# A two-layer hybrid attention and FFN kernel: tile addresses set apart modulo 128 bytes, query-key products alternated between row halves, the first compression matrix used unsplit, and another opening order

## The chip, the cores and the metric

The kernel runs on one core of a Trainium2 chip. The metric is the device time of one execution in microseconds, taken as the median over several runs. The profile is of one execution on the chip; PE is TensorE's matmul row, PEld its weight loads, DVE VectorE, ACT ScalarE, POOL GpSimd and SP SyncE.

## The reference, cut to what matters

Two layers act on 256 tokens of width 1024, in float32:

```python
for l in range(DEPTH):
    h = rmsnorm(x, norm_mix_g[l]); proj = h @ w_in[l]
    # a: 24 heads of 64 in three dilation groups, banded causal attention, merged by log-sum-exp
    out_a = dilated_mixer(qa, ka, a_qkv[:, :, 2])
    # b: keys and values compressed over 32 tokens: gelu(flat @ cmp_w1) @ cmp_w2
    out_b = nsa_mixer(qb, k_cmp, v_cmp, k_sel, v_sel, k_win, v_win, b_gate)
    gate = sigmoid(merge)
    x = x + (gate0 * (out_a @ w_proj_a[l]) + gate1 * (out_b @ w_proj_b[l])) @ w_out[l]
    h = rmsnorm(x, norm_ffn_g[l]); g_in, u = split(h @ w_up[l])
    x = x + (silu(causal_dwconv(g_in, ...)) * u) @ w_down[l]
```

`cmp_w1[l, kv]` is a 2048 x 256 matrix for the keys (kv = 0) and one for the values (kv = 1). The output is the last x.

## The kernel before, in words

All weights lie in one stream of 512 KB halves; two halves are a unit (L42 lists the units in their order). SP loads each half into one of five `raw` tiles (L204, L206). For a unit, ACT casts the half to float32r as `hi` (L232) and DVE subtracts to get `lo` (L233). Activations are split in the same way, so that a product is three float32r matmuls: hi by hi, lo by hi, hi by lo (`mm3`, L283, and `feat_major`, L358). Each has its own weight load (PEld) of 128 columns. PE runs its program in the order in which the code emits it.

The input projections (`chunk_in`, L434) load tokens of `hT` as weights and stream 512 columns (280 in chunk c11) of the unit: 24 matmuls a unit, as L284, L285 and L286. The merge units (L927), both `proj` products (L972 to L974), `out_proj` (L985), `ffn_up` (L1001) and `ffn_down` (L1051) load the unit's columns as weights and stream 256 tokens: 48 matmuls a unit (L936 to L938, L972 to L974, L363, L1062 to L1064). A layer has 9 chunks c0 to c8 and c10, c11, bq of two units each, 8 merge, 4 proj, 4 out, 22 up, 11 down and 4 compression (w1) units.

Attention is written as generators (`job_a`, `job_b`, `job_cmp1`, `job_cmp2`, `rope_run`) that `tick` (L268) moves on by one step after each half of a projection unit, so that their instructions fall between the projections' matmuls. `chunk_in` calls `post_fn`, which starts `rope_run`, then `tick`. In `rope_run` (L411) the key path yields twice (L420) before the scaling by POOL's power (L368); its `fin` transposes the result on PE (`rope_b`, L474 after the copy L471).

`job_a` (L589) computes for head `lo` (partitions 0 to 63) all query-key products (`qk`, L606: L608, L609, L614), yields, takes the masked maxima on DVE (L603), and then does the same for head `up` (partitions 64 to 127). `col_pair` (L556) multiplies probabilities by values for two heads in turn, which write to PSUM partitions 0 to 63 and 64 to 127 (L560).

`job_cmp1` (L763) builds the compression input `Fv`, splits it into `F` (hi and lo side by side), and `w1_unit` (L793) multiplies F by hi and lo of each w1 unit: 16 matmuls of 256 columns a unit (L806, L807), four units a layer, placed after units 5, 6, 8 and 10 of the chunks.

The opening (L1072 on): SP issues gain, x in three parts and the halves of unit 0, then in `attention_layer` misc, ropec, cossin, gr, post, w2t; then the next halves. `feed` (L299) permutes each 128-token half of a feature block of x into token order, scales it into `hT` (two ACT instructions L310, two DVE L311), squares it (ACT L314, L317) and adds the square to a sum (POOL L319). Before the second unit of c10, `rstd_col` (L331) is emitted, whose matmul L334 needs the finished sum (`fin`, L327).

**Addresses.** The pools hand out SBUF in the order in which tiles are first asked for, each size rounded up to 32 bytes. Adding them up: `hT`, `raw`, and the `hi` and `lo` tiles of the shared pool `com` begin 96 bytes past a multiple of 128, `oTb` too; `oTa` at 0; the FFN's `u` and `act` at 32. In the FFN every third unit (`ffn_turn`, L209) takes `hi` and `lo` from the FFN's pool, at 32; the others take those of `com`, at 96. So the weight tile and the streamed tile of a matmul begin 64 bytes apart modulo 128 in two of three FFN units, 32 apart with `oTa`, and at the same place everywhere else.

The key line of each part:

```python
hi = pool.tile([P, UW], F32R, name="hi", bufs=nb)          # L222, com or the FFN's pool
T.matmul(s1[:, c0:c0 + P], qT[r, g, tok], kT[r, g, tok], start=True, stop=True)   # L614
T.matmul(o, F[:, c0:c0 + P], hi[:, j], start=jj == 0, stop=False)                # L806
```

## Time and profile before

| | us |
|---|---|
| median of 3 runs | 1004.22 (1000.14 to 1005.84) |
| the profiled execution's own time | 1000.91 |
| its span, first to last instruction | 999.2 |
| PE busy | 972.5 (97%) |
| DVE busy | 772.7 (77%) |
| ACT busy | 603.6 (60%) |
| POOL busy | 147.4 (15%) |

A row of a timeline has the start in us, the length in us of the merged run, engine, line, operation, `out<-in`, shapes and the count; in brackets the idle time of the engine before it and what ended it. The end of a matmul is modelled, so rows overlap: the time that a matmul takes from the engine is read from start to start. A window's row has each engine's busy time, the granted TensorE clock as a share of 2.4 GHz, the DMA share and GB/s.

### The profile page before, as it was taken

Reading aid. Unit: us, or ns where it says so; the run is one execution under the profiler, and the core shown is the slowest. Engines: PE = TensorE matmul, PEld = TensorE weight load, DVE = VectorE, ACT = ScalarE, POOL = GpSimd, SP = SyncE. Lnnn points to the kernel's source line nnn. Section 1 sums busy time; section 2 is a strip of 40 time slices with the busy share of each in tenths; the row PEclk is TensorE's granted clock in tenths of the full one; section 3 lists DMA queues with packets and bytes.
Section 4 is the critical chain, followed back from the end, with each engine's and each line's share of the span. In section 5 each row is a group of like instructions: output and inputs, shape, how many; then the busy total and the mean of one; then the engine's idle time right before and its main releaser. Section 6 shows DMA issues by size and latency. Waiting matters only on the chain.

```text
span 999.2 us, 18707 instructions
## 1 busy us (share of the span) xinstructions
PE 972.5 (97%) x7154; PEld 894.0 (89%) x7154; DVE 772.7 (77%) x1628; ACT 603.6 (60%) x1219; POOL 147.4 (15%) x164
## 2 busy tenths in 40 slices
PE   5899999999999999999998999999999999999998
PEld 3778888888999999999987788888899999999998
DVE  6799777887679898886478987787875898988742
ACT  6779666758456555555456886675665555555531
POOL 2241111203002111110112300121210021111100
PEclk9999999999999999999998999999999999999999
DMA  6644345534356566555454433563354465565660
GB/s 206 209 150 146 130 148 190 168 108 148 127 170 212 174 205 193 189 187 193 160 162 148 148 127 128 172 208 109 103 177 160 148 226 179 186 195 190 196 205 22
DMA packets 47897, 164.90 MB, mean 165 GB/s; under 512 B 6080, under 2 KB 7616, under 8 KB 47808
## 3 DMA queue, kind: packets, MB, share of 16 engines
q1 hardware_dynamic: 46656, 162.66, 50.1%
q8 instruction: 56, 0.92, 0.4%
q10 hardware_dynamic: 1152, 1.05, 0.3%
q14 instruction: 33, 0.27, 0.1%
HBM read 162.64 MB, written 1.05 MB: 164 GB/s over the span
## 4 chain that ended last, share of the span: by engine, by line
PE 81%; DVE 10%; ACT 6%; issue 2%; POOL 1%; DMA 1%; SPq 0%; DVEq 0%; ACTq 0%; POOLq 0%
PE acc L363 25%; PE acc L284 6%; PE acc L286 6%; PE acc L285 6%; PE acc L1062 4%; PE acc L1064 4%; PE acc L1063 4%; DVE lo L233 3%; PE acc L936 3%; PE acc L938 3%; PE att L560 3%; PE acc L937 3%; PE att L565 2%; PE acc L972 2%; PE acc L973 2%
## 5 line engine op out<-in xcount | busy, mean ns | idle before, releaser
L233 DVE TENSOR_TENSOR lo<-raw,hi 128x1024 fp32r<-128x1024 f32 (+1 forms) x308 | 386.3, 1274 | 62.6 <-ACT hi L232 60.7
L232 ACT CAST hi<-raw 128x1024 fp32r<-128x1024 f32 (+1 forms) x308 | 310.2, 1039 | 176.8 <-issue 49.2
L363 PE MATMUL acc<-u,hi 128*128 128x256 f32 x1376 | 240.9, 279 | 0.0
L363 PEld LDWEIGHTS acc<-u,hi 128*128 128x128 f32 x1376 | 210.0, 189 | 0.1
L363 PE MATMUL acc<-u,lo 128*128 128x256 f32 x688 | 191.8, 279 | 0.0
L284 PE MATMUL acc<-hi,hT 128*128 128x512 f32 (+1 forms) x384 | 154.7, 403 | 9.4 <-ACT hi L232 9.4
L286 PE MATMUL acc<-lo,hT 128*128 128x512 f32 (+1 forms) x384 | 151.2, 394 | 0.7 <-DVE lo L233 0.5
L285 PE MATMUL acc<-hi,hT 128*128 128x512 f32 (+1 forms) x384 | 150.2, 391 | 0.0
L363 PEld LDWEIGHTS acc<-u,lo 128*128 128x128 f32 x688 | 130.1, 189 | 0.0
L1064 PE MATMUL acc<-act,lo 128*128 128x256 f32 x352 | 97.8, 278 | 0.0
L1063 PE MATMUL acc<-act,hi 128*128 128x256 f32 x352 | 97.8, 278 | 0.0
L1062 PE MATMUL acc<-act,hi 128*128 128x256 f32 x352 | 97.8, 278 | 0.0
L284 PEld LDWEIGHTS acc<-hi,hT 128*128 128x128 f32 x384 | 73.8, 192 | 23.5 <-ACT hi L232 9.4
L286 PEld LDWEIGHTS acc<-lo,hT 128*128 128x128 f32 x384 | 73.8, 192 | 17.9 <-DVE lo L233 3.2
L285 PEld LDWEIGHTS acc<-hi,hT 128*128 128x128 f32 x384 | 73.9, 192 | 13.0 <-issue 0.3
L936 PE MATMUL acc<-hT,hi 128*128 128x256 f32 x256 | 74.3, 290 | 0.0
L938 PE MATMUL acc<-hT,lo 128*128 128x256 f32 x256 | 72.7, 284 | 0.0
L937 PE MATMUL acc<-hT,hi 128*128 128x256 f32 x256 | 72.3, 282 | 0.0
L1062 PEld LDWEIGHTS acc<-act,hi 128*128 128x128 f32 x352 | 66.5, 189 | 0.0
L1064 PEld LDWEIGHTS acc<-act,lo 128*128 128x128 f32 x352 | 66.5, 189 | 0.0
L1063 PEld LDWEIGHTS acc<-act,hi 128*128 128x128 f32 x352 | 66.5, 189 | 0.0
L1034 POOL TENSOR_TENSOR z<-z,rb 128x512 f32<-128x512 f32 x22 | 30.5, 1386 | 207.2 <-DVE z L1033 207.2
(212 smaller groups left out, 1783.9 us busy)
## 6 DMA issues: line engine op xcount, KB each, us to landing
raw<-in_ws_dram SPq DMA_DIRECT2D x300, 512.0 KB, 4.5
raw<-in_ws_dram SPq DMA_DIRECT2D x8, 280.0 KB, 4.3
out_dram<-x ACTq DMA_DIRECT2D x8, 128.0 KB, 2.2
gr<-in_g_rope_dram SPq DMA_DIRECT2D x2, 384.0 KB, 5.7
masks<-in_mask_dram SPq DMA_DIRECT2D x1, 576.0 KB, 4.9
x<-in_x_dram SPq DMA_DIRECT2D x2, 256.0 KB, 4.3
x<-in_x_dram SPq DMA_DIRECT2D x1, 512.0 KB, 7.5
w2t<-in_w_dram SPq DMA_DIRECT2D x2, 128.0 KB, 4.8
```

Source lines behind the costliest of these rows:

```text
L232: A.copy(h, r)
L233: V.tensor_sub(l, r, h.bitcast(F32))
L284: T.matmul(o, a_hi, b_hi, start=first, stop=False)
L285: T.matmul(o, a_lo, b_hi, start=False, stop=False)
L286: T.matmul(o, a_hi, b_lo, start=False, stop=last)
L363: return [lambda a=a: T.matmul(a[0], a[1], a[2], start=a[3], stop=a[4]) for a in todo]
L936: T.matmul(o, hi[:, k, ms], hT[:, 0, k], start=k == 0, stop=False)
L937: T.matmul(o, hi[:, k, ms], hT[:, 1, k], start=False, stop=False)
L938: T.matmul(o, lo[:, k, ms], hT[:, 0, k], start=False, stop=k == 7)
L1062: T.matmul(ps, hi[:, c], act[:, 0, k], start=k == 0, stop=False)
L1063: T.matmul(ps, hi[:, c], act[:, 1, k], start=False, stop=False)
L1064: T.matmul(ps, lo[:, c], act[:, 0, k], start=False, stop=k == NFT - 1)
```

## The change

1. **Addresses.** `warm` is added, misc is widened from 72 to 96 floats, mhalf is asked for after the `raw` tiles, `db` gets six buffers, `pad` tiles of 64 bytes are added, some tiles are asked for in another order, and the scratch at the foot of SBUF shrinks to 1024 bytes. Added up in the same way, all of these streams begin at multiples of 128: `hT`, `raw`, `u`, `act`, `oTa`, `oTb`, `qS`; `hi` and `lo` of both pools and `kS` begin at 64 past one.
2. **Query-key products.** They alternate between the two row halves, matmul by matmul; the own-group products come first, the dilated ones after a yield.
3. **First compression matrix.** A w1 unit now holds four row blocks of both matrices. It is not split: its float32 `raw` halves are streamed (256 columns) against the unsplit `F` with 32 columns as weights; four matmuls write to four 32-partition blocks of one PSUM tile.
4. **Opening.** The host gives a second copy of x in permuted token order (`xo`); `feed` reads it without a permutation, with one ACT and one DVE instruction a block; the squares of blocks 0 to 3 go to POOL. xo is issued ahead of gain, unit 1's halves right after the last part of xo; x itself (1 MB) after masks. A first activation on `warm` comes at the start. The halves of unit 0 are converted between the blocks. The tables (`tabs`, `tabc`) are multiplied on POOL.
5. **Order in `chunk_in` and `rope_run`.** `rstd_col` comes after the first 12 matmuls of c10's second unit, in both layers; the key path yields three times.

```diff
+    warm = com.tile([P, 32], F32, name="warm")
+    G.memset(warm, 0.0)
+    A.activation(warm, warm, AF.Square)
...
-    mhalf = com.tile([P, 16], F32, name="mhalf")
-    G.memset(mhalf, -0.5)
-    misc = com.tile([P, 72], F32, name="misc")
+    misc = com.tile([P, 96], F32, name="misc")
...
+            if u[0] == "w1":
+                split[i] = [load_half(i, c0, UW // 2) for c0 in (0, UW // 2)]
+                nxt[0] += 1
+                continue
...
+        sq = sums["acc"] if m == 0 else com.tile([P, S], F32, name="sq", bufs=2)
+        if src is not x and m < 4:
+            G.tensor_tensor(sq, xm, xm, op=ALU.mult)
+        else:
+            A.activation(sq, xm, AF.Square)
...
         for a in range(2):
-            V.tensor_tensor(tabs[:, a], cossin[:, a, :, None, :].to_broadcast([P, 2, 5, 64]),
+            G.tensor_tensor(tabs[:, a], cossin[:, a, :, None, :].to_broadcast([P, 2, 5, 64]),
...
-            for _ in range(2 if ksc is None else 0):
+            for _ in range(3 if ksc is None else 0):
...
-                if c == "c10" and kh == 1:
-                    nrm["col"] = rstd_col()
...
                     if kh == 1:
+                        if c == "c10" and t == 0:
+                            nrm["col"] = rstd_col()
                         post_fn(t, ps[t])
...
+            def qk_dil():
+                s1 = [att(), att()]
                 for half in range(2):
                     tok = slice(half * P, (half + 1) * P)
                     for g in (1, 2):
                         c0 = (2 * half + g - 1) * P
-                        T.matmul(s1[:, c0:c0 + P], qT[r, g, tok], kT[r, g, tok], start=True, stop=True)
-                return s0, s1
+                        for a in range(2):
+                            T.matmul(s1[a][:, c0:c0 + P], qT[rows[a], g, tok], kT[rows[a], g, tok],
+                                     start=True, stop=True)
+                return s1
...
-            ss = qk(lo)
-            yield
-            all_max(0, *ss)
-            ss = qk(up)
-            yield
-            all_max(1, *ss)
+            ss = qk_seq()
+            yield
+            max_seq(ss)
+            ss = qk_dil()
+            yield
+            max_dil(ss)
...
-            d = pool.tile([P, 2, 2, 2], F32, name="db", bufs=3)
+            d = pool.tile([P, 2, 2, 2], F32, name="db", bufs=6)
...
+        pad = pool.tile([P, 16], F32, name="pad")
+        G.memset(pad, 0.0)
+        oT["a"] = big("oTa", "bigA")
...
-                fr = hps["F"][:, kv]
-                split_evac(fr[:, :, 0:32], fr[:, :, 32:64], Fv.rearrange("p j h c -> p j (h c)"))
-                Fc[kv] = fr
+                Fc[kv] = Fv
...
-            for j in range(8):
-                jj = uh * 8 + j
-                c0 = 64 * (15 * kv + jj)
-                T.matmul(o, F[:, c0:c0 + P], hi[:, j], start=jj == 0, stop=False)
-                T.matmul(o, F[:, c0:c0 + P], lo[:, j], start=False, stop=jj == 15)
+            for jp, half in enumerate(next_unit()):
+                wv = half.rearrange("p (u v n) -> p u v n", u=2, v=2)
+                for kv in range(2):
+                    for u in range(2):
+                        r = 64 * kv + 32 * u
+                        jj = 4 * w + 2 * jp + u
+                        T.matmul(ps[r:r + 32, 0:256], hps["F"][:, kv, jj].rearrange("p h c -> p (h c)"), wv[:, u, kv],
+                                 start=jj < 2, stop=jj >= 14)
...
             nc.sync.dma_start(masks, mask_c)
+            nc.sync.dma_start(x, x_in.rearrange("p (k q) -> p k q", k=8))
...
+    with tc.tile_pool(name="start", bufs=1, reuse_waits="tile") as pool:
+        xo = pool.tile([P, 8, S], F32, name="xo")
+        xv = xo_in.rearrange("p (k q) -> p k q", k=8)
+        nc.sync.dma_start(xo[:, 0:2], xv[:, 0:2])
+        nc.sync.dma_start(gain, g_norm.rearrange("p (a k) -> p a k", k=8))
+        early[0, 0] = load_half(0, 0, UW // 2)
+        mhalf = com.tile([P, 16], F32, name="mhalf")
+        G.memset(mhalf, -0.5)
+        nc.sync.dma_start(xo[:, 2:4], xv[:, 2:4])
+        early[0, UW // 2] = load_half(0, UW // 2, UW // 2)
+        nc.sync.dma_start(xo[:, 4:8], xv[:, 4:8])
+        early[1, 0] = load_half(1, 0, UW // 2)
+        early[1, UW // 2] = load_half(1, UW // 2, UW // 2)
+        for m in range(8):
+            if m in (1, 3):
+                if m == 1:
+                    prepare(0)
+                pend.popleft()[1]()
+            feed(hT, m, 0, False, xo)
...
-            hT = out_proj(l, pool, mT)
+            u = new_u(pool, "u")
             act = pool.tile([P, 2, NFT, S], F32R, name="act")
+            pad = pool.tile([P, 16], F32, name="pad")
+            G.memset(pad, 0.0)
+            hT = out_proj(l, u, mT)
...
-    nc = _bacc.Bacc("TRN2", target_bir_lowering=False, num_devices=1)
+    nc = _bacc.Bacc("TRN2", target_bir_lowering=False, num_devices=1, dynamic_dma_scratch_size=1024)
```

## Rows read from the trace of the kernel before

**Rows 1.** The page, busy time by engine, and the chain that ended last

```profile
PE 972.5 (97%) x7154; PEld 894.0 (89%) x7154; DVE 772.7 (77%) x1628; ACT 603.6 (60%) x1219; POOL 147.4 (15%) x164
...
PE 81%; DVE 10%; ACT 6%; issue 2%; POOL 1%; DMA 1%; SPq 0%; DVEq 0%; ACTq 0%; POOLq 0%
```

**Rows 2.** Windows by stage: PE, PEld, DVE, ACT, POOL busy, clock, DMA

```profile
0.00:12.00 12.00, 2.51 (x5) 1.60 (x6) 4.27 (x7) 7.18 (x14) 1.97 (x10) 1.00 0.77 258
...
30.00:60.00 30.00, 26.47 (x139) 21.88 (x140) 26.60 (x64) 22.50 (x39) 9.09 (x6) 1.00 0.53 171
60.00:110.00 50.00, 49.24 (x312) 40.53 (x310) 45.27 (x164) 41.93 (x127) 11.26 (x13) 1.00 0.43 138
...
320.00:444.00 124.00, 123.66 (x1063) 123.40 (x1062) 108.00 (x144) 69.17 (x93) 15.38 (x12) 1.00 0.59 190
```

**Rows 3.** Timeline of PE in ffn_down, first matmuls of three successive units

```profile
449.12 0.28 PE L1062 MATMUL acc<-act,hi 128*128 128x256 f32 x1
...
454.56 0.28 PE L1062 MATMUL acc<-act,hi 128*128 128x256 f32 x1
...
460.32 0.28 PE L1062 MATMUL acc<-act,hi 128*128 128x256 f32 x1
```

**Rows 4.** Timeline of PE in a projection unit, then in a merge unit

```profile
79.74 0.39 PE L285 MATMUL acc<-hi,hT 128*128 128x512 f32 x1
...
80.42 0.39 PE L285 MATMUL acc<-hi,hT 128*128 128x512 f32 x1
...
86.13 0.29 PE L938 MATMUL acc<-hT,lo 128*128 128x256 f32 x1
...
87.57 0.28 PE L938 MATMUL acc<-hT,lo 128*128 128x256 f32 x1
```

**Rows 5.** Groups by line and form: count, busy us, mean ns, idle before

```profile
L284 PE MATMUL acc<-hi,hT 128*128 128x512 f32 x352 | 145.1, 412 | 9.4 <-ACT hi L232 9.4
...
L936 PE MATMUL acc<-hT,hi 128*128 128x256 f32 x256 | 74.3, 290 | 0.0
...
L363 PE MATMUL acc<-hT,hi 128*128 128x256 f32 x256 | 46.6, 285 | 0.0
```

**Rows 6.** Timeline of PE, one query-key step of job_a and what follows

```profile
166.99 0.48 PE L608 MATMUL att<-qkT 64*128 64x128 f32 x2
167.31 0.59 PE L609 MATMUL att<-qkT 64*128 64x256 f32 x2
...
168.73 0.50 PE L284 MATMUL acc<-hi,hT 128*128 128x512 f32 x1
```

**Rows 7.** Timeline of PE, one col_pair of job_a and what follows

```profile
195.21 1.09 PE L560 MATMUL att<-pT,vA 128*64 128x256 f32 x12
196.22 0.55 PE L565 MATMUL att<-ident,pt 128*128 128x128 f32 x3
```

**Rows 8.** Timeline of PE, one w1 unit, first matmul and what follows

```profile
156.35 0.36 PE L806 MATMUL att<-hi,F 128*128 128x256 f32 x1
...
158.34 0.40 PE L284 MATMUL acc<-hi,hT 128*128 128x512 f32 x1
```

**Rows 9.** Timeline of all engines in the first 40 us

```profile
4.80 1.28 ACT L310 ACT_TABLE_LOAD   x1 [4.80 <-DMA x<-in_x_dram]
...
9.45 0.79 PE L284 MATMUL acc<-hi,hT 128*128 128x512 f32 x1 [9.45 <-ACT hi L232]
...
15.10 0.74 POOL L319 TENSOR_TENSOR acc<-acc,sq 128x256 f32<-128x256 f32 x1 [0.41 <-ACT sq L317]
...
16.24 1.11 POOL L319 TENSOR_TENSOR acc<-acc,sq 128x256 f32<-128x256 f32 x1 [0.39 <-ACT sq L317]
...
20.00 0.68 PE L334 MATMUL att<-ones,fin 128*128 128x1 f32 x4 [2.21 <-DVE fin L327]
```

**Rows 10.** Timeline of PE, the first key transposes of both layers

```profile
39.95 0.44 PE L474 MATMUL att<-ident,rd 128*128 128x128 f32 x2 [2.52 <-DVE rd L471]
...
527.45 0.69 PE L474 MATMUL att<-ident,rd 128*128 128x128 f32 x2 [2.72 <-DVE rd L471]
```

More of the change, by code (lines that the diff above doesn't have):

```diff
@@ L50, in layer_units @@
                 w = W1_AT.index(2 * c + kh)
-                units += [("w1", w // 2, w % 2)]
+                units += [("w1", w)]
         if c in MERGE_AT:
@@ L93, in pack_stream @@
             elif u[0] == "w1":
-                a = tiles(np.asarray(inp["cmp_w1"][l, u[1]])[u[2] * 1024:(u[2] + 1) * 1024])
+                w1 = np.asarray(inp["cmp_w1"][l]).reshape(2, 16, P, 256)[:, 4 * u[1]:4 * u[1] + 4]
+                a = w1.transpose(2, 1, 0, 3).reshape(P, UW)
             elif u[0] == "merge":
@@ L163, in block_kernel @@
 @with_exitstack
[L164 removed]
+def block_kernel(ctx, tc, x_in, xo_in, ws, g_norm, g_rope, pos, w2, conv, rope_c, ropec_c, mask_c, misc_c, out):
     nc = tc.nc
@@ L297, in new_u, with feed @@
         return u
-    def feed(u, m, gi, natural):
-        xm = x[:, m]
+    def feed(u, m, gi, permute, src=None):
+        src = x if src is None else src
+        xm = src[:, m]
         gc = gain[:, gi, m:m + 1]
-        if natural:
+        if not permute:
             A.activation(u[:, 0, m], xm, AF.Copy, scale=gc)
@@ L321, in feed @@
         fin = com.tile([P, S], F32, name="fin", bufs=1)
-        if natural:
+        if not permute:
             V.tensor_add(fin, sums["acc"], sq)
@@ L391, in attention_layer, with big @@
         qscB = pool.tile([P, 2, 8], F32, name="qscB")
+        qS = pool.tile([P, 2, 4, S], F32R, name="qS")
+        bigF = pool.tile([P, 2, 16, 2, 16], F32, name="F", tag="bigF", bufs=1)
+        def big(n, tag):
+            t = pool.tile([P, 2, 4, S], F32R, name=n, tag=tag, bufs=1)
+            return t
         gs = pool.tile([P, 2, 3, 8], F32, name="gs")
+        kS = pool.tile([P, 2, 4, S], F32R, name="kS")
         vB = pool.tile([P, 2, 2, P], F32, name="vB")
@@ L604, in maxes, with qk_seq @@
                                        scalar=-3e38, op0=ALU.add, op1=ALU.max, accum_out=mx[:, a, m:m + 1])
-            def qk(r):
-                s0, s1 = att(), att()
-                T.matmul(s0[:, 0:P], qT[r, 0, 0:P], kT[r, 0, 0:P], start=True, stop=True)
-                T.matmul(s0[:, P:P + S], qT[r, 0, P:S], kT[r, 0, :], start=True, stop=True)
+            def qk_seq():
+                s0 = [att(), att()]
+                for q0, k1, c0 in ((0, P, 0), (P, S, P)):
+                    for a in range(2):
+                        T.matmul(s0[a][:, c0:c0 + k1], qT[rows[a], 0, q0:q0 + P], kT[rows[a], 0, 0:k1],
+                                 start=True, stop=True)
+                return s0
+            def qk_dil():
+                s1 = [att(), att()]
                 for half in range(2):
@@ L613, in qk, with max_seq, max_dil @@
                         c0 = (2 * half + g - 1) * P
[L614 to L627 removed]
+                        for a in range(2):
+                            T.matmul(s1[a][:, c0:c0 + P], qT[rows[a], g, tok], kT[rows[a], g, tok],
+                                     start=True, stop=True)
+                return s1
+            def max_seq(s0):
+                for a in range(2):
+                    pt = pool.tile([P, 896], F32, name="pt", bufs=4)
+                    pts.append(pt)
+                    maxes(s0[a], a, 0, 0, P, qscA[:, 0, hp, 0, a:a + 1], 0)
+                    maxes(s0[a], a, P, P, S, qscA[:, 1, hp, 0, a:a + 1], 3)
+            def max_dil(s1):
+                for a in range(2):
+                    for half in range(2):
+                        for g in (1, 2):
+                            i = 2 * half + g - 1
+                            maxes(s1[a], a, i * P, 384 + i * P, P, qscH[:, half, hp, g - 1, a:a + 1], 3 * half + g)
+            ss = qk_seq()
             yield
[L629 to L630 removed]
+            max_seq(ss)
+            ss = qk_dil()
             yield
[L632 removed]
+            max_dil(ss)
             V.tensor_copy(mx[up, :, 6:7], mx[up, :, 0:1])
@@ L681, in job_a @@
             yield
-            if "a" not in oT:
-                oT["a"] = big("oTa", "bigA")
             res = pool.tile([P, S], F32, name="res", bufs=1)
@@ L778, in job_cmp1 @@
                         A.copy(by_residue(T2[64 * u:64 * u + 64, :, c0:c0 + P], t), src[64 * u:64 * u + 64])
-                Fv = pool.tile([P, 16, 2, 16], F32, name="Fv", tag="pt", bufs=4)
+                if kv == 0:
+                    hps["F"] = bigF
+                Fv = hps["F"][:, kv]
                 G.memset(Fv[:, :, :, 15:16], 0.0)
@@ L810, in w1_unit @@
             hid = pool.tile([P, 256], F32, name="hid", bufs=1)
-            A.copy(hid[0:64], ps[0:64, 0:256])
-            A.copy(hid[64:128], ps[64:128, 256:512])
+            A.copy(hid, ps[:, 0:256])
             hps["hid"] = hid
@@ L983, in attention_layer, with out_proj @@
         return mT
-    def out_proj(l, pool, mT):
-        u = new_u(pool, "u")
+    def out_proj(l, u, mT):
         for m in range(4):
@@ L1068, in ffn_down @@
             else:
-                feed(u, m, 2 * l + 2, False)
+                feed(u, m, 2 * l + 2, True)
         return u
     hT = new_u()
-    xv = x_in.rearrange("p (k q) -> p k q", k=8)
-    nc.sync.dma_start(gain, g_norm.rearrange("p (a k) -> p a k", k=8))
-    nc.sync.dma_start(x[:, 0:2], xv[:, 0:2])
-    early[0, 0] = load_half(0, 0, UW // 2)
-    nc.sync.dma_start(x[:, 2:4], xv[:, 2:4])
-    early[0, UW // 2] = load_half(0, UW // 2, UW // 2)
-    nc.sync.dma_start(x[:, 4:8], xv[:, 4:8])
-    for m in range(8):
-        feed(hT, m, 0, False)
-        if m == 1:
-            prepare(0)
-            flush(0)
+    with tc.tile_pool(name="start", bufs=1, reuse_waits="tile") as pool:
[17 more added lines that the diff above has]
+            feed(hT, m, 0, False, xo)
     for l in range(DEPTH):
```

37 lines of the change are left out of this document (7 added, 30 removed).

## The prediction

> **What bounds the kernel now.** I read the page first: PE is busy 97% of the span and makes 81% of the chain that ended last; DVE has 77% [rows 1]. So what shortens PE's stream shortens the time, as long as DVE keeps up. The windows say where that is in doubt: between 30 and 110 us DVE is busy 89 to 91%, in the FFN's up stage 87% (108.0 of 124), and from 30 to 60 us PE already idles 3.5 of 30 us [rows 2]. A busy PE is not yet a PE at its best, so I went on to starts. In `ffn_down`, 48 matmuls of one unit take from 449.12 to 454.56, 5.44 us or 113.3 ns each; the same 48 of the next unit take 5.76 us, 120.0 ns each [rows 3]. Nothing differs but the weights' pool: the slower unit has `hi` and `lo` at 32 past a multiple of 128, as `act` is, the quicker at 96. Merge units, with both streams at 96, go at 120 ns (1.44 us for 12), and the projections' 512-column matmuls at 227 ns (0.68 us for 3) [rows 4]. At the clock's upper level, 2.4 GHz, 256 columns would need 107 ns and 512 columns 213. So equal addresses modulo 128 cost about 13 ns a matmul, 64 apart about 7, whatever the number of columns.
>
> **The change, part by part.**
>
> *Addresses.* A matmul that moves from equal addresses to 64 apart should lose 120.0 - 113.3 = 6.7 ns [rows 3]. Counts, over both layers: projections 1056 with 512 columns (three lines of 352) and 96 with 280; merges 768 (three of 256); `out_proj` 384 (the row shows 256 of its hi lines, lo is half of that) [rows 5]; `oTb` 192 by the code (2 units of 48 a layer); every third unit of the FFN, 16 up and 6 down units of 48, 1056. That is 3552 x 6.7 ns = 23.8 us. The 192 of `oTa`, now 32 apart, I give half, 0.6 us, and some 256 of the first up units and of `job_b` 1.4 us. Sum 25.8 us. For the 512-column form the 6.7 is carried over, not seen: its excess over 213 is 14 ns, that of the 256-column form at equal addresses 13, so I take the same half. Bounds: nothing at the bottom; at the top all 5856 such matmuls at 107 ns and 213 ns, another 6.6 ns each, 38 us more. I take the middle, which has a row of its own. All pairs that go to 64 apart are now at multiples of 64, where before they were 32 off; no row shows such a pair.
>
> What the row shows, then, is a streaming matmul slowed by the place of its weights. The Trainium skill (TensorE: Matmul & The Clock Gate, Part 2, step-by-step) says that PE has two independent SBUF read ports and that loading the next weights doesn't steal read bandwidth from the running matmul. By that rule this part would be worth nothing; the 113.3 against 120.0 ns speaks against it.
>
> *Query-key products.* One step for one head half runs from 166.99 to 168.73, 1.74 us [rows 6], and `job_a` has two, in 8 jobs: 27.9 us. Each of its six products shows as two records. About 0.2 us of a step lies in entering and leaving the 64-row form (L608 to L609 takes 0.32 for two records of 128 columns), and there remain two steps a job. The nearest row for two halves at once is `col_pair`: 12 records, four of 256 columns and eight of 128, take 1.01 us [rows 7]; one after the other, at 2.4 GHz and two passes over the columns, they would take 4 x 213 + 8 x 107 = 1.7 us. So column halves overlap almost wholly. If row halves do too, 1.54 us of each 1.74 halves: 8 x 1.54 = 12.3 us. Bounds 0 and 12.3; I take 11, since the 128-column loads may not overlap as well as the 64-column ones of the row. DVE's maxima stay the same in number (4 after the first products and 8 after the second, instead of 6 and 6), and the PSUM tiles in use stay two.
>
> *First compression matrix.* One w1 unit takes 1.99 us on PE, 156.35 to 158.34 [rows 8]; 8 units make 15.9 us. After: 8 float32 products a unit, 16 records of about 0.213 us. One after the other that is 3.4 us a unit, 27 us in all, a loss of 11; two at a time 13.6 and 1.5 of changing forms, a gain of 1; four at a time 6.8 and 1.5, a gain of 7.5. Rows 7 show two at a time at full speed and nothing on four; the records are then issued in the same way to two more column blocks, so I take 6. Besides, 16 halves lose their cast and subtraction, and `F` its split. This unloads ACT and DVE, not PE; I give it nothing of its own, it pays for the friction below. The raw halves are now held until PE has read them, so SP's stream of `raw` waits for PE twice in a row; three of five tiles are left, and PE reads them right after the unit before, hence 0. If that cover is gone, the next unit's cast comes late.
>
> *Opening.* The 1.28 us table load stands ahead of ACT's first work, and PE's first matmul waits for ACT until 9.45 [rows 9]; the early activation takes the load off that path. `rstd_col` after 12 matmuls (2.7 us at 227 ns) covers PE's 2.21 us wait for `fin` [rows 9]. That is 3.5 us, and fewer ACT and DVE instructions a block add some; unit 1's halves overtake six small transfers on SP. Against it: `gr` lies, with `tabs`, where `xo` was, so its transfer waits until the last block is read, and post, w2t and c11's halves queue behind it; x's 1 MB behind masks takes 4 us of the transfers at 258 GB/s [rows 2], ahead of bq's second unit; and by 30 us DVE is near its limit. Squares and tables on POOL run beside DVE: a POOL addition took 0.74 us, and 1.11 us beside DVE's table product [rows 9]. I take 4 us; bounds 0 and 7.
>
> The Trainium skill (SBUF — State Buffer, Who interferes with whom) says that a DVE instruction with two SBUF inputs contends with a GpSimd instruction that reads SBUF, and that the later waits. The stretched POOL addition agrees; by that rule the moved work costs DVE a little time and doesn't free all of it.
>
> *The third yield.* PE waits 2.52 and 2.72 us for the copy L471 ahead of the first key transposes, once a layer [rows 10]. One more tick puts 12 matmuls, 2.7 us, in between. I take 4 of the 5.2 us (bounds 0 and 5.2): what is late next is the rest of the key path, and then the b jobs, which begin one tick later while PE has chunk work. The pads and the moved tiles cost a memset each on POOL, which is busy 15%; in the FFN the memset waits for `oTa`, whose last reader ends before POOL's next task. Nothing.
>
> *Sum.* 25.8 + 11 + 6 + 4 + 4 = 50.8 us. Between 30 and 110 us, and in the same stretch of layer two, DVE has a tenth to give and PE's gain there is about 4 us a layer; I take 4 us off as friction: 46.8. The profiled execution took 1000.9 us, so 954 by its own time. The median of the runs, 1004.2, stands 3.3 above it; I forecast 956 for the median.
>
> **The rivals.**
>
> *Nothing from addresses.* The two speeds in rows 3 come from something else that goes with the pool, or the tiles don't land where I add them up to. For it: no row has both streams at multiples of 64. Against: merges, from another pool, show the same 120 at equal addresses. Time 956 + 26 = 982; if the compression products also go one at a time, 17 more, 999. Chance 0.13, of it 0.02 for the latter. The rule of the Trainium skill on the two read ports (TensorE: Matmul & The Clock Gate, Part 2) would give 982, too.
>
> *Lined up costs nothing.* Off by 32, both streams may cut a step of 64 bytes in two; at multiples of 64 the remaining 7 ns would go as well. For it: 32 apart and 0 apart differ, so finer steps than 128 matter. Against: no row. Half to all of the 38 us: about 925. Chance 0.13.
>
> *DVE or the transfers become the bound.* In 30 to 110 us and its like in layer two, DVE at 90% keeps PE's gain, and the opening gains nothing since x's extra MB and `gr` hold up the weights. Lost: 4 of the opening, 4 of the yields, 6 in those stretches: 970. For: rows 2. Against: DVE loses 16 subtractions and the splits of `F`. Chance 0.12.
>
> *Slower.* What counts is not the distance modulo 128 but the distance in a longer period, which the smaller scratch and the new order shift for all pairs. Then the pairs may as well lose 6.7 ns as gain it: 5856 x 6.7 = 39 us up, against 21 from the rest: about 1020. It decides from 3.6 ns more per matmul than now (21 / 5856). For: I have two distances and no more. Against: `u` and `act`, `hT` and `oTb` lie far apart and show the same 120.0. Chance 0.04.
>
> **How the numbers follow.** The forecast holds with 0.58, and the four rivals with 0.13, 0.13, 0.12 and 0.04. The range runs from 932 to 984: it holds the forecast with the bounds of the query-key and compression terms, the supply case and most of the case without addresses, and leaves out the lined-up case's greater part and the slower one, under 0.2. A measurement of this kernel can tell about 0.5%, 5 us, from no change. Faster by more: everything but the slower case and the case at 999, 0.94. Within: 0.02. Slower: 0.04.
>
> **What would show it.** Right: in every FFN unit 48 matmuls take 5.44 us, merges go at 113 ns, projections at 220; query-key records come in pairs a few ns apart, and a step of both heads takes about 1 us; a w1 unit takes about 1.05 us and L232 and L233 have 16 fewer instructions; PE's first matmul starts before 8.2 us (9.45 less 1.28), and the idle time ahead of L334 and L474 is gone. Wrong: 120 and 227 ns stand as they were; the query-key records still follow 110 ns apart; w1 records 213 ns apart singly; new idle time of PE behind L232, L233 or `raw`, above all in the first 60 us.

## The result: 974.2 us, three fifths of the gain that was forecast

The kernel after took 974.18 us in the median of 4 runs (971.18 to 974.93), the kernel before 1003.56 on the same chip (1000.14 to 1005.84): a ratio of 0.9704, 95% interval 0.9669 to 0.974. The forecast was 956, its range 932 to 984. So the direction and the range hold, but of 46.8 us some 29 came. The profiled execution took 974.93 us with a span of 973.1. The mean granted clock was 0.993 in the trace before and 0.992 in the trace after, so the clock is no part of the difference between the two.

The page of the kernel after, busy time by engine, and the chain that ended last:

```profile
PE 949.1 (98%) x7154; PEld 860.4 (88%) x7154; DVE 753.5 (77%) x1593; ACT 580.7 (60%) x1186; POOL 156.4 (16%) x179
...
PE 80%; DVE 10%; ACT 6%; issue 2%; DMA 1%; POOL 1%; SPq 0%; DVEq 0%; ACTq 0%; POOLq 0%
```

PE is still the bound, in nearly the same share as in [rows 1]: 23.4 us fewer of busy PE in a span 26.1 us shorter. The windows of the kernel after:

```profile
0.00:12.00 12.00, 4.23 (x9) 2.18 (x9) 5.50 (x7) 6.63 (x11) 5.89 (x15) 1.00 0.79 256
...
20.00:30.00 10.00, 7.58 (x37) 6.54 (x36) 7.93 (x18) 5.63 (x14) 6.04 (x6) 0.83 1.00 363
30.00:60.00 30.00, 28.62 (x147) 23.38 (x147) 26.86 (x60) 22.06 (x40) 6.04 (x4) 1.00 0.62 211
```

PE starts earlier, and between 30 and 60 us it idles 1.4 us instead of 3.5 [rows 2]. But from 20 to 30 us it idles 2.4 us, with the transfers at a share of 1.00 and the granted clock at 0.83 in the mean, a part of the stretch at the lower of its two levels, 1.2 GHz.

**Where the time came from.** I added up, for every matmul of both traces, the time from its start to the start of the next one. The projections with 512 columns fell from 268.7 to 266.7 us, up from 246.8 to 244.6, merges and `out_proj` from 143.8 to 137.7, down from 121.8 to 119.8, and `oTa` with `oTb` rose from 46.2 to 46.8: 11.7 us less for all long stretches together. Query-key products fell from 28.6 to 18.5, w1 from 16.0 to 8.0. Against that, c11's products with 280 columns rose from 14.4 to 18.2.

PE's starts in `ffn_down` of the kernel after, first matmuls of two successive units, the answer to [rows 3]:

```profile
436.54 0.28 PE L1082 MATMUL acc<-act,hi 128*128 128x256 f32 x1
...
441.98 0.28 PE L1082 MATMUL acc<-act,hi 128*128 128x256 f32 x1
```

48 matmuls take 5.44 us, 113.3 ns each, and so does every unit of down: this step came. In the up stage it didn't come everywhere. First matmuls of three successive units there, PE's timeline:

```profile
338.41 0.28 PE L373 MATMUL acc<-u,hi 128*128 128x256 f32 x1
...
344.06 0.39 PE L373 MATMUL acc<-u,hi 128*128 128x256 f32 x2
...
349.50 0.28 PE L373 MATMUL acc<-u,hi 128*128 128x256 f32 x1
```

The sixth unit takes 5.65 us (117.8 ns a matmul), the seventh 5.44. In both layers the first six go at 117.8 and all others at 113.3. Projections and merges, PE's timeline, the answer to [rows 4]:

```profile
84.72 0.28 PE L957 MATMUL acc<-hT,hi 128*128 128x256 f32 x1
...
86.08 0.28 PE L957 MATMUL acc<-hT,hi 128*128 128x256 f32 x1
...
88.44 0.40 PE L290 MATMUL acc<-hi,hT 128*128 128x512 f32 x1
...
89.13 0.40 PE L290 MATMUL acc<-hi,hT 128*128 128x512 f32 x1
```

This merge has 1.36 us for 12, 113.3 ns (others stand at 117.8). The projections have 0.69 us for 3, 230 ns, where they had 227: they became slower, not quicker.

The second half of a query-key step and a w1 unit, PE's timeline, the answers to [rows 6, 8]:

```profile
163.05 1.16 PE L632 MATMUL att<-qkT 64*128 64x128 f32 x16
164.14 1.07 PE L827 MATMUL att<-raw,F 128*32 128x256 f32 x16
165.15 0.50 PE L290 MATMUL acc<-hi,hT 128*128 128x512 f32 x1
```

Eight products of 128 columns for both heads take 1.09 us, a w1 unit 1.01. Both are as forecast.

What PE waits for in the whole trace (waited-for instruction: us in total, times, longest):

```profile
PE acc L290 <- ACT hi L238: 8.1, 3, 7.4
PE acc L292 <- DVE lo L239: 4.8, 7, 2.2
PE att L485 <- DVE rd L482: 2.6, 2, 1.8
PE att L344 <- DVE fin L333: 1.8, 2, 0.9
PE att L795 <- DVE cdup L792: 1.8, 2, 1.5
PE att L621 <- ACT qkT L548: 1.2, 1, 1.2
```

The wait for the first matmul fell from 9.45 us [rows 9] to 7.42, that for the key transposes from 5.2 us [rows 10] to 2.6, the 2.2 us for `fin` are gone. But the waits for `lo` rose from 0.5 to 4.8 us. The row of the kernel before:

```profile
PE acc L286 <- DVE lo L233: 0.5, 2, 0.3
```

Apart from the first matmul, all waits of this view sum to 13.1 us, against 13.7 before: as much waiting as the reordering removed came back at other places.

### The profile page after: what moved, and what is told of

It is laid out like the page before. It is cut to its first block, busy times and chain, and to the rows that moved or that the text cites. A ratio compares the mean times of both kernels' runs of the same rounds, so it can differ in the third digit from the quotient of the medians.

```text
span 973.1 us, 18637 instructions
## 1 busy us (share of the span) xinstructions
PE 949.1 (98%) x7154; PEld 860.4 (88%) x7154; DVE 753.5 (77%) x1593; ACT 580.7 (60%) x1186; POOL 156.4 (16%) x179
## 4 chain that ended last, share of the span: by engine, by line
PE 80%; DVE 10%; ACT 6%; issue 2%; DMA 1%; POOL 1%; SPq 0%; DVEq 0%; ACTq 0%; POOLq 0%
PE acc L373 25%; PE acc L290 6%; PE acc L292 6%; PE acc L291 6%; PE acc L1084 4%; DVE lo L239 4%; PE acc L1083 4%; PE acc L1082 4%; PE att L571 3%; PE acc L957 3%; PE acc L959 3%; PE acc L958 3%; PE att L576 2%; ACT pt L664 2%; PE acc L993 2%
## 5 line engine op out<-in xcount | busy, mean ns | idle before, releaser
L239 DVE TENSOR_TENSOR lo<-raw,hi 128x1024 fp32r<-128x1024 f32 (+1 forms) x292 | 368.0, 1278 | 54.7 <-ACT hi L238 51.7
L238 ACT CAST hi<-raw 128x1024 fp32r<-128x1024 f32 (+1 forms) x292 | 293.8, 1037 | 161.1 <-PE acc L291 41.3
L373 PE MATMUL acc<-u,hi 128*128 128x256 f32 x1376 | 237.7, 278 | 0.0
L290 PEld LDWEIGHTS acc<-hi,hT 128*128 128x128 f32 x384 | 74.0, 193 | 26.1 <-ACT hi L238 10.2
```

The lines of the kernel that those rows point to most:

```text
L238: A.copy(h, r)
L239: V.tensor_sub(l, r, h.bitcast(F32))
L290: T.matmul(o, a_hi, b_hi, start=first, stop=False)
L373: return [lambda a=a: T.matmul(a[0], a[1], a[2], start=a[3], stop=a[4]) for a in todo]
```

## The experiments

**What distance does: PE alone.** m1 and m2 hold stretches of matmuls with nothing beside them.

> Only matmuls on two tiles, in stretches of one distance between the start of the weights and of the stream, modulo 128 bytes, in steps of 16, with 256 and with 512 columns, the tiles at 0 and at 32; the layers are left out, and the output is x. Theory A (the distance decides): 256 columns at distance 0 take 120 ns from start to start and at 64 take 113 or 118, the two values that the changed kernel shows; 512 columns take 227 at distance 0 and 230 at 64, and some other distance is quicker than both. Rival B (the place in the kernel decides: other engines' reads and writes of SBUF beside PE): with nothing beside PE, all distances take the same time, near 107 to 110 ns and 213 to 216. If tiles at 0 and at 32 agree, the absolute place doesn't matter.

> This kernel leaves out the layers: it holds only stretches of matmuls in the form of this kernel's products (128 x 128 weights; 256 columns, 48 to a stretch, or 512 columns, 24 to a stretch) with nothing on the other engines beside them, and writes its input back. In one part each stretch follows three transposes, and the distance between weights and stream runs from 0 to 480 bytes in steps of 32. In the other part the distance is 64 or 0 bytes, and each stretch follows a few products of another kind: two with half the rows, two pairs with both row halves, four with half the columns, four with 16 columns, or an idle time. Theory (the distance counts modulo 256 bytes, not 128): 256 columns take 120.0 ns at 0 and 256, about 117.8 at 64, 192, 320 and 448, and at 128 and 384 neither the one nor the other but 118 to 119; 512 columns take 226.7 ns at 0 and 256, about 229 at 64 and 192, 231 to 233 elsewhere. Theory on the 113.3 ns that units of the FFN show at 64 bytes: a stretch is entered in one of two phases, and at least one of the other kinds ahead of it gives 113.3 at 64 and 120.0 at 0. Rival (the period is 128): 128, 256 and 384 all take 120.0 and 226.7. Rival for 113.3 (it comes from what the other engines do meanwhile): no kind of entry gives under 117.

Mean ns from start to start in the second half of each stretch of m2, by the distance in bytes of the two operands (with 256 columns of the weights behind the stream, with 512 of the stream behind the weights):

```
distance      0     32     64     96    128    160    192    224    256    320    448
256 cols  120.0  118.3  113.3  117.3  118.5  120.0  117.8  116.7  120.0  113.3  117.8
512 cols  226.7  233.3  228.9  233.3  232.6  234.3  233.3  233.3  226.7  228.9  233.3
```

Both rows repeat after 256 bytes, not 128: 64 and 192 differ, 0 and 128 too. And the two forms want different places: 256 columns are quickest 64 apart, 512 columns at equal addresses, where the kernel before had them. m1 had shown 120.0 and 226.7 at equal addresses and 117.8 and 228.8 at 64, and at these two distances no difference between both operands at 0 and both at 32 off: being lined up costs or gains nothing there, and no other engine is needed for the slow speeds. In the second part of m2 the same distance of 64 gives two speeds by what went ahead. PE's timeline there (`alt`: row halves in pairs ahead; `short`: four products of 16 columns ahead):

```profile
292.97 5.72 PE L86 MATMUL n256d64altr<-mt,wt 128*128 128x256 f32 x48
298.53 5.66 PE L86 MATMUL ahead<-mt,wt 128*128 128x512 f32 x24
...
315.76 0.51 PE L62 MATMUL entry<-mt,wt 128*128 128x16 f32 x4
316.12 5.90 PE L86 MATMUL n256d64shortr<-mt,wt 128*128 128x256 f32 x48
321.86 5.76 PE L86 MATMUL ahead<-mt,wt 128*128 128x512 f32 x24
```

From start to start the first stretch has 5.56 us, the second 5.74; from one matmul to the next 113.3 and 117.8 ns, to the last. Row halves, column halves, transposes or an idle time ahead gave 113.3, the four short products 117.8, in both repetitions. At equal addresses all kinds gave 120.0. The kind of product ahead doesn't settle it alone: m1 had 117.8 at this same distance behind one or two transposes, where m2 has 113.3 behind three.

**e1: the addresses alone.** The kernel before with the new layout only:

```
-    mhalf = com.tile([P, 16], F32, name="mhalf")
...
     early[0, 0] = load_half(0, 0, UW // 2)
+    mhalf = com.tile([P, 16], F32, name="mhalf")
...
+            pad = pool.tile([P, 16], F32, name="pad")
+            G.memset(pad, 0.0)
```

> The kernel before with the addresses alone changed (weights 64 apart from the streams everywhere); all else as before. If the address part is worth what the starts in the changed kernel show, 12 us of 1000 are gained (ratio 0.988): up units and down units at 113, merges and proj at 114 to 118, projections no quicker at 230. The prediction's 25.8 us would give 0.974. A rival in which the addresses are worth nothing and all comes from the other parts gives 1.000.

993.85 us, ratio 0.9912 (0.9884 to 0.994), about 9 us. Where nothing breaks in, 512 columns rose from 229.2 to 229.7 ns; up, merges and down fell. This is the size of the address part, a third of the 25.8 forecast.

**e2: weights moved again.** The kernel after with `mhalf` and `pad` 64 bytes longer; the two `rstd` buffers grow by 32 bytes each, so that the tiles of attention and FFN keep their place modulo 128:

```
-        r = com.tile([P, 3, 2], F32, name="rstd", bufs=2)
+        r = com.tile([P, 8, 2], F32, name="rstd", bufs=2)
...
-        mhalf = com.tile([P, 16], F32, name="mhalf")
+        mhalf = com.tile([P, 32], F32, name="mhalf")
...
-            pad = pool.tile([P, 16], F32, name="pad")
+            pad = pool.tile([P, 32], F32, name="pad")
```

> The changed kernel with the weight copies back at a multiple of 128, all else as changed. If distance decides, 256-column units go back to 120 ns and projections to 227 ns, and the time rises by about 14 us over the changed kernel (ratio to the kernel before 0.984). If lined-up tiles were the point of the address part, it stays at the changed kernel's time (0.970).

991.71 us, ratio 0.9898 (0.9867 to 0.9929), 17.5 above the kernel after, where 14 were expected. By the period of 128 this is the same place again, and 120.0 and 227 were to come; the trace shows 118.7 and 232.4 ns. First matmuls of two successive units of up:

```profile
360.49 0.28 PE L373 MATMUL acc<-u,hi 128*128 128x256 f32 x1
...
366.18 0.28 PE L373 MATMUL acc<-u,hi 128*128 128x256 f32 x1
```

Modulo 256 the distance is 128, and m2 has 118.5 and 232.6 there. So the period of 256 holds inside the kernel.

**e3: the tables on DVE.** `G.tensor_tensor(tabs...)` and `tabc` as `V.tensor_tensor`.

> The changed kernel with the rope tables multiplied on DVE again, as before; all else as changed. Theory: in the changed kernel the table products on POOL from 20.3 us on hold up three small DVE instructions (1.54 and 2 of 1.05 us in place of 0.17 and 0.24), and c11's lo halves come late, for which PE idles 2.2 us at 24 us. With the tables on DVE, DVE has 1.8 us more to do, but those three take their old time: PE's idle time ahead of c11 shrinks by 1 to 2 us, and the time by as much (ratio to the kernel before 0.968 to 0.970). Rival: the halves are late because of their transfers behind gr; then nothing changes, or the 1.8 us of DVE add to the time (0.970 to 0.973).

970.48 us, ratio 0.9687 (0.9663 to 0.9711): within the intervals not told from the kernel after, but the traces differ at one place. The kernel after around 20 us, all engines:

```profile
20.28 3.10 POOL L394 TENSOR_TENSOR tabs<-cossin,gr 128x640 f32<-128x640 f32 x2
20.33 1.54 DVE L348 TENSOR_SCALAR rstd<-rstd 128x2 f32<-128x2 f32 x1 [0.59 <-POOL rstd L347]
...
21.79 2.10 DVE L351 TENSOR_SCALAR dg<-ident,rstd 128x128 f32<-128x128 f32 x2
...
26.11 0.40 PE L292 MATMUL acc<-lo,hT 128*128 128x280 f32 x1 [2.18 <-DVE lo L239]
```

And e3's DVE:

```profile
19.66 1.55 DVE L394 TENSOR_TENSOR tabs<-cossin,gr 128x640 f32<-128x640 f32 x2
...
21.33 0.16 DVE L348 TENSOR_SCALAR rstd<-rstd 128x2 f32<-128x2 f32 x1
21.40 0.47 DVE L351 TENSOR_SCALAR dg<-ident,rstd 128x128 f32<-128x128 f32 x2
```

Beside POOL's table products DVE's three small instructions take 3.64 us, without them 0.63. POOL needs 3.10 us for what DVE does in 1.55. So PE stood 2.18 us for a `lo` that DVE made late; in e3 that wait is gone, and the products with 280 columns take 15.1 us instead of 18.2. The wait is not all of it. Behind it the granted clock of the kernel after falls to 1.2 GHz; in e3 it stays at 2.4 GHz:

```profile
28.00:30.00 2.00, 2.00 (x10) 2.00 (x9) 1.12 (x3) 1.60 (x3) 1.39 (x1) 0.50 0.96 399
```

```profile
20.00:30.00 10.00, 9.12 (x63) 8.43 (x62) 8.06 (x28) 7.83 (x17) 3.12 (x3) 1.00 0.98 364
```

The first row is the kernel after, the second e3, whose row stands against the 0.83 of the kernel after from 20 to 30 us. A mean of 0.83 over 10 us is 1.7 us of PE's work, beside the 2.18. The Trainium skill (SBUF — State Buffer, Who interferes with whom) lists tensor_scalar among the instructions that can take the port pair shared with GpSimd, and says that who issues first holds it; the two columns of `rstd` at 1.54 us beside L394 agree.

**e4: query-key products head after head**, in the kernel after:

```
-            ss = qk_seq()
+            ss = qk(lo)
...
-            ss = qk_dil()
+            ss = qk(up)
```

> The kernel after, but the query-key products of the two heads one head after the other, as before. Theory (alternated row halves overlap, and this gave 10 us on PE's own path): the time rises by 10 us over the kernel after, ratio to the kernel before 0.980 to 0.982; records of the query-key products are again about 110 ns apart. Rival (DVE's maxima set the pace of these jobs, or the order changes the speed of the long stretches behind them): it rises by less than 5 us, or by over 13, and the long stretches behind the products change their pitch.

983.55 us, ratio 0.9823 (0.98 to 0.9846), 9.4 us above the kernel after: the theory holds. The group's start-to-start sum is 28.8 us again. A side gain was not seen: up and down have the pitch of the kernel after.

**e5: the first compression matrix split again**, in the kernel after:

```
-            if u[0] == "w1":
-                split[i] = [load_half(i, c0, UW // 2) for c0 in (0, UW // 2)]
...
+                split_evac(fr[:, :, 0:32], fr[:, :, 32:64], Fv.rearrange("p j h c -> p j (h c)"))
```

> The kernel after, but the first compression matrix split into two halves of half precision each and multiplied as before. Theory (eight PE units of 1.0 us where there were 2.0, and DVE's and ACT's saved work is hidden): the time rises by 8 us, ratio 0.978 to 0.980. Rival (the saved casts and subtractions count as well, since DVE is busy for nine tenths of these stretches): it rises by 11 us or more, ratio 0.981 and over, with new idle time of PE in the first 60 us and its like in layer two.

988.40 us, ratio 0.9868 (0.9848 to 0.9887), 14.2 above the kernel after: the rival holds. PE's w1 products rose by 7.4 us. The waits of PE in e5 show part of the rest:

```profile
PE acc L285 <- ACT hi L233: 12.4, 4, 7.3
PE acc L287 <- DVE lo L234: 5.3, 4, 2.2
PE att L339 <- DVE fin L328: 2.9, 2, 1.5
```

Without the first wait of 7.3 us, the casts are late by 5.1 us instead of 0.7 (the first row). At the first block of the 512-column projections with index 0, ahead of any w1 unit, e5 is already 3.1 us later (50.01 against 46.89 us): there `F` is split on ACT and DVE. And at the start of each layer's up stage the wait for `fin` is 1.5 us, where the kernel after has 0.9 at most; right behind it the granted clock falls in e5 and not in the kernel after. Windows around the first of these, e5 and then the kernel after:

```profile
313.00:333.00 20.00, 18.54 (x144) 18.28 (x143) 15.91 (x29) 10.64 (x17) 3.43 (x4) 0.91 0.60 196
```

```profile
307.00:327.00 20.00, 19.13 (x161) 18.88 (x161) 16.15 (x28) 9.81 (x16) 5.52 (x4) 1.00 0.66 213
```

A mean of 0.91 over 20 us is 1.8 us of PE's work, and layer two shows the same. So the saved casts and subtractions did count, in waits and in clock; how much of the clock's part each run has can't be told from one trace, for in e3 a wait for `fin` of 1.54 us had no fall of the clock behind it.

**e6: tables on DVE and x later.** As e3, and x's transfer after the fourth block of the input stage.

> The kernel after with the tables' products on DVE, and x's transfer issued after the fourth block of layer one's input stage instead of ahead of it. Theory (x's 1 MB holds up the weights for the projections' last units, and PE waited 2.2 us for them at 24 us): 1 to 3 us less than the kernel with the tables on DVE alone (970.5), ratio 0.966 to 0.968. Rival (the weights are late because of their own casts, not of the transfers): within 0.5 us of that kernel, ratio 0.969.

972.23 us, ratio 0.9709 (0.9691 to 0.9726); the theory falls, since this is no less than e3's 970.48. With x issued at 40.93 us instead of 20.66, the transfers' share from 20 to 30 us is still 0.98 (e3: 0.98), so x's 1 MB is neither what fills them nor what PE waits for.

**e7: every stretch of 256 columns at 64 modulo 256.**

```
-        rb = com.tile([P, S], F32, name="rb", bufs=1)
+        rb = com.tile([P, S + 32], F32, name="rb", bufs=1)[:, :S]
```

> The kernel after, with 128 bytes of padding ahead of the attention's and the FFN's tiles, so that in every matmul of 256 columns in the long stretches the weights stand 64 bytes behind the stream modulo 256. In the kernel after that holds for the merges and every third unit of the FFN only; for both halves of the attention's output projections and the rest of the FFN it is 192. Theory (the period is 256; at 64 a stretch is at 113.3 ns after products of almost every other kind, at 192 it falls into 117.8, and a stretch hands its phase to the next): some 1440 of these matmuls go from 117.8 to 113.3, 6.5 us, so 967 to 969, ratio 0.963 to 0.965; the projections' 512 columns stay at 229 to 231. Rival (192 and 64 are the same, as the forecast's period of 128 had it): no difference from the kernel after, 0.970.

979.59 us, ratio 0.9762 (0.9715 to 0.9809), no faster than the kernel after, where 967 to 969 were expected. But its six runs are 971.56, 972.34, 979.09, 980.10, 983.32 and 985.91, 14.4 us apart. The granted clock doesn't explain that: the runs of 972.34 and of 985.91 us both have a mean of 0.991. The profiled one was the quickest, and there every unit of up and down is at 113.3 ns, the first six too:

```profile
320.35 0.28 PE L373 MATMUL acc<-u,hi 128*128 128x256 f32 x1
...
325.79 0.28 PE L373 MATMUL acc<-u,hi 128*128 128x256 f32 x1
```

**e8: besides, 512 columns at equal addresses, tables on DVE.** The halves for the input projections start 192 bytes further in their tiles:

```
+            o = 48 if u[0] == "in" else 0
+            hi = pool.tile([P, UW + 64], F32R, name="hi", bufs=nb)[:, o:o + UW]
```

> As the run with all stretches of 256 columns at 64, and besides the halves of the input projections' weights 192 bytes further into their tiles, so that weights and stream of the products with 512 columns stand at the same place modulo 256, as in the kernel before; and the tables' products on DVE. Theory: 1056 products of 512 columns go from about 230.0 to 226.7 ns, 3.5 us, and the tables give 2 to 4 us, so 960 to 963, ratio 0.957 to 0.960. Rival (the speed of a stretch hangs on what runs beside it, not on the distance): the 512 columns stay at 230, and the time is no more than 4 us under that of the other run.

971.46 us, ratio 0.9721 (0.9669 to 0.9773), above the 960 to 963 expected, and again spread, from 967.56 to 981.60. The 512 columns show 227 ns from the thirteenth product of an unbroken stretch on (229 before the move), but the mean start-to-start time of all that follow one another directly falls only from 230.1 to 229.3, since other products break most of these stretches up after twelve. The theory's 3.5 us were 0.8.

**e9: the opening of before**, in the kernel after (no early activation, squares on ACT, permuted reads, tables on DVE, the column statistic ahead of its 24 matmuls, no second transfer of x):

```
-    A.activation(warm, warm, AF.Square)
...
+        feed(hT, m, 0, True)
```

> The kernel after with the opening of before: no early activation, the squares on ACT, the input in its own order and read through the permutation, the second unit's halves not early, the tables on DVE, the column statistic ahead of its 24 matmuls, no second transfer of the input. Theory (the opening's gain at the first matmul, 2.0 us, and at the wait for the column sum, 2.2 us, is given back by 3.8 us of waiting for the second block's weights): within 1 us of the kernel after, ratio 0.969 to 0.972; the first matmul at 9.4 us, and no idle time of 2 us ahead of the second block's low halves. Rival (the forecast's 4 us hold and the waiting at 24 us comes from elsewhere): 978, ratio 0.974 to 0.975, with that idle time still there.

976.15 us, ratio 0.9735 (0.9705 to 0.9765), 2.0 above the kernel after, 3 by the ratios: between theory and rival, and the intervals overlap. The traces say more. At the first block of the projections with index 0 e9 is 4.5 us behind (51.40 against 46.89 us). From 51 us to the end of layer one it stays some 3.6 to 3.7 behind (188.35 against 184.71 us, 506.12 against 502.39), but for a stretch from 190 us on, which is the clock's doing. The kernel after and e9:

```profile
190.00:200.00 10.00, 10.00 (x45) 8.37 (x45) 4.89 (x17) 2.70 (x7) 0.00 (x0) 0.66 0.24 90
```

```profile
190.00:200.00 10.00, 10.00 (x73) 8.79 (x69) 6.47 (x15) 2.92 (x7) 0.00 (x0) 0.83 0.45 144
```

The kernel after loses 3.4 us there and e9 1.7; at the start of the up stage e9 loses as much again, behind a wait for `fin` of 1.6 us, and is 3.7 us behind once more. In layer two the kernel after waits 1.52 us for `cdup`, e9 0.40, and 2.6 us are left at the end. So through layer one the opening gains about what was forecast, with its tables on POOL. With the tables on DVE in both, e3 against e9, the ratios are 0.9687 and 0.9735, some 4.8 us.

**e10: e7 and four short products.** A test of whether e7's spread is the two speeds of m2:

```
+                if c == 1:
+                    t16 = att()
+                    for i in range(4):
+                        T.matmul(t16[:, 16 * i:16 * i + 16], u[:, 0, i, 0:P], u[:, 0, i, 0:16], start=True, stop=True)
```

> The kernel with all 256-column stretches at 64, and four more products with 16 columns, whose result isn't used, ahead of the third unit of each layer's up stage. Theory (at 64 a stretch goes at 113.3 or 117.8 ns by the phase in which it is entered and hands that on until other work breaks in; the spread of 971.6 to 985.9 us among that kernel's runs comes from stages in either phase): the four products turn the phase as they did by themselves, the remaining 20 units of up and the 11 of down in each layer go at 117.8, 2976 products by 4.5 ns make 13 us over the quick runs, so 983 to 987 in nearly every run, the spread gone. Rival (the phase recovers within a unit or two, and the spread has another cause): the units stand at 113.3 again soon after, and the times spread from 971 to 986 as without the four products.

985.18 us, all five runs from 982.62 to 986.98; ratio 0.9833 (0.9808 to 0.9858). PE's timeline of e10, the four products and the units after them:

```profile
317.47 0.51 PE L1068 MATMUL att<-u 128*128 128x16 f32 x4
317.83 0.48 PE L373 MATMUL acc<-u,hi 128*128 128x256 f32 x2
...
323.57 0.28 PE L373 MATMUL acc<-u,hi 128*128 128x256 f32 x1
...
329.22 0.28 PE L373 MATMUL acc<-u,hi 128*128 128x256 f32 x1
...
481.86 0.28 PE L1086 MATMUL acc<-act,hi 128*128 128x256 f32 x1
...
487.51 0.28 PE L1086 MATMUL acc<-act,hi 128*128 128x256 f32 x1
```

5.65 us a unit from 323.57 on, and still 5.65 in the last units of down, 164 us later; layer two goes the same way. Half a microsecond of short products makes the span 11.0 us longer than e7's traced one (980.8 against 969.8), although the mean granted clock is higher (0.998 against 0.995), and the spread is gone. The theory holds. That e7's longer runs also had stages at 117.8 is argued from their times, which reach the same 986; only the shortest was traced.

## Why the prediction was right, and where it was wrong

**Addresses: the step that failed.** The forecast said "A matmul that moves from equal addresses to 64 apart should lose 120.0 - 113.3 = 6.7 ns", with 25.8 us for all. About 9 came by e1, 11.7 by the traces. Three things went wrong in it.

1. "For the 512-column form the 6.7 is carried over, not seen" (1056 of 3552, 7.1 us). Its sign was wrong: 64 apart costs this form 2.2 ns and more (m1 and m2, 228.9 or 233.3 for 226.7).
2. Distances were counted modulo 128. Added up modulo 256, `u` and `act` against `com`'s halves and both `oT` stand at 192 in the kernel after, not at 64. At 192 the transposes led m2 to 117.8, and both `oT` show 117.8. But `u` and `act` against `com`'s halves stood at 192 before the change, too, and that is the quick unit of [rows 3]: 192 also has 113.3. So this mistake cost little: with all pairs at 64 (e7) the traced span is 3.3 us shorter than that of the kernel after, and some 2 us of that go with the higher granted clock (0.995 against 0.992).
3. One speed was taken per distance. There are two, 113.3 and 117.8, and a stretch hands its own to the next: from `oTa` (751 us in layer two) through `out_proj` to the sixth unit of up all stand at 117.8.

The range held because "nothing" was its lower bound for this term; that 974 lies in it doesn't bear out the 25.8.

**Query-key products: right.** Forecast 11, in the sums 10.1, undone 9.4.

**First compression matrix: right on PE, wrong beside it.** Forecast 6, from 15.9 to some 8.3 with the changes of form; PE's sum fell by 8.0, since four column blocks run wholly at once. "I give it nothing of its own" was the mistake: undoing it costs 14.2, 7.4 of it in PE's products, so the unloading of ACT and DVE was worth some 6 more in this order of work. In the traced run about 3.6 of these are the two falls of the clock behind longer waits.

**Opening: right in size, but for the tables.** The first matmul starts 2.0 us earlier and `fin`'s 2.2 us are gone. Against e9 the gain is 4.5 us at the end of the opening, some 3.7 through layer one and 2.6 at the end; forecast was 4. The cost of POOL beside DVE was named and given "a little time": it was 3 us of DVE, 2.18 of PE's waiting, and 1.7 through the clock that fell behind that wait. The prediction had no term for the clock.

**Third yield: half.** 2.6 of the 5.2 us are left; forecast was 1.2. No run undid this part alone.

**Friction of 4: too low.** The parts, e1's by itself and the others by their undoing, sum to 9 + 9.4 + 14.2 + 2 = 35 us and more with the third yield, the whole is 29. That what one part gives PE is taken by another's waits for DVE fits the waits, 13.7 us before and 13.1 after, but it is argued; no run shows which wait took what. The sum itself gives 1004.2 - 46.8 = 957.4 for the median; the 956 written is 1.4 below it.

**The rivals.** "Nothing from addresses" falls by e1, m1 and m2; "Lined up costs nothing" by m1, where both operands lined up or both 32 off go alike at distances 0 and 64. "DVE or the transfers become the bound" named 970, near what came, but its mechanism is a small part: PE's waits are the same in total, and x's transfer, moved in e6, holds nothing up; `gr`'s was not moved in any run. "Slower" had the longer period right, for which I gave 0.04, and its price wrong: I had held against it that tiles far apart show the same 120.0, but before the change the pairs whose addresses I compared are, added up, all equal modulo 256, too, so that row could not tell.

**Open.** What sets the two speeds at one distance was not found, only one thing that turns them. In the kernel after, every third unit of the FFN is at 64 and the others at 192, and its runs lie within 4 us of each other; perhaps the change of distance lets the 113.3 come back, as it does after the sixth unit, but no run tried this by itself. No version run here is faster than e3 beyond its interval.

## What to carry to other kernels

Where long runs of back-to-back matmuls don't go at the pace of the clock, plot the start-to-start time against the distance of the two operands in SBUF, for each width separately and over at least 256 bytes, before a layout is changed; a speed seen at one width says nothing of another. Products that use half of the rows, or a quarter of the columns, belong side by side in the order of issue: both gave what the arithmetic says. And when an engine with a tenth of its time to spare is relieved or burdened, price that too: here it was worth nearly as much as PE's own part, and a good part of it came through the granted clock, which in several traces fell right behind a longer wait of PE.

## What was not expected of the hardware

- Start-to-start times of these matmuls depend on the operands' distance modulo 256 bytes: 113.3 to 120.0 ns with 256 columns, 226.7 to 234.3 with 512, with the best places at 64 and at 0 (m2); in the FFN of the kernel before, pairs at 192 reach 113.3, too. The Trainium skill (TensorE: Matmul & The Clock Gate, Part 2, step-by-step) has independent read ports for the two and no read bandwidth taken from the running matmul; the rows of m2, which differ by the distance alone, don't agree.
- At 64 apart there are two speeds, 113.3 and 117.8, and four products of 16 columns brought in the slower one, which then held for 164 us of PE work (e10).
- Two elements a partition took DVE 1.54 us beside a POOL product, and 0.16 without (e3).
- Right behind waits of PE of 2.18 us (kernel after) and 1.5 us (e5) the granted clock fell to 1.2 GHz, which cost 1.7 and 1.8 us beside the wait; behind a wait of 1.54 us in e3 it did not fall.
